# Splitting queries, keys and values into 16-bit halves where they leave PSUM, and turning the keys by DMA when they are loaded

## The chip, the cores and the metric

The kernel runs on one core of one Trainium2 chip. The time is the device time of one execution in microseconds; the kernel before has a median of 2367.46 us over three runs (2366.59 to 2371.02).

## What is computed

One inference step of a decoder with two layers. Layer 0 (the "even" layer) projects the normalised input with one matrix and feeds two mixers with four heads each: a gated linear recurrence (HGRN2, "A") and forgetting attention ("B"). Layer 1 (the "odd" layer) is another gated recurrence (GLA, "C"). There is a prompt of 2048 tokens and a sample of 8 x 4 tokens with a paged cache. The change is in B, for the prompt:

```python
def fox_prompt(q, k, v, log_f):          # (1, 2048, 4 heads, 128)
    c = jnp.cumsum(log_f, axis=1).swapaxes(1, 2)
    def block(args):                     # 128 queries at a time
        qi, ci, s0 = args
        logits = jnp.einsum('bthd,bshd->bhts', qi, k) * scale + ci[..., None] - c[:, :, None, :]
        logits = jnp.where(t[:, None] >= key_pos[None, :], logits, -jnp.inf)
        p = jax.nn.softmax(logits, axis=-1)
        return jnp.einsum('bhts,bshd->bthd', p, v)

def even_mixer(h, w_in, ...):
    qa, fa, ia, ga, qb, kb, vb, gb, fb = _split(h @ w_in, ...)
    o_a, s_a = gated_linear_chunked(...)            # A
    o_b = fox_attend(hb(qb), kb_h, vb_h, log_fb) * jax.nn.silu(gb)   # B
    return jnp.concatenate([o_a, o_b], axis=-1) @ w_out, ...
```

The keys and values kb and vb are outputs too, in float32.

## The kernel before

**Products of two halves.** Float32 data goes through TensorE as two float16 halves: hi = f16(x) and lo = f16(x - hi), scaled by powers of two. A product is three matmuls, hi·hi, hi·lo and lo·hi (`mm3`, lines 595 to 597). Whoever makes an operand must write both halves; `split_evac`, for example, writes hi on ScalarE (ACT) and lo on VectorE (DVE).

**The even layer.** It runs in two halves of 1024 tokens (`hf`; the first takes the 32 sample tokens along). A half is a list of 16 units of the input projection in the order v0, g0, qf0, qf1, Bq0, Bg0, v1, g1, qf2, qf3, Bq1, Bg1, Bk0, Bv0, Bk1, Bv1. A unit holds 256 columns of weights (two heads; Bv0 has four more columns and so a PSUM tile for each 128 tokens instead of one for two). The recurrence of one head (`lin`) is woven between units by `mux`: head 0 beside units 3 and 4, head 1 beside 5 to 7, head 2 beside 9 and 10, head 3 beside 11 to 13, that is Bg1, Bk0 and Bv0. While units 14 and 15 of the first half run, the next half's input is normalised and turned by DMA transposes (L511).

- `mk_bq` (Bq): the projection gives q transposed, head dimension on the partitions, in segments of 352 tokens (first half) or 512 (second). ScalarE copies a segment with the scale `fsc` from PSUM (L990), and SP stores it as float32 to `qTd` in DRAM.
- `mk_bkv` (Bk, Bv): tokens on the partitions. VectorE scales two tiles of 128 tokens into a float32 tile `t` (L1019), which SP stores as the output (L1033). Values are stored a second time to `vd` (L1036). For keys TensorE turns `t` with four transposes (L1044), ScalarE copies them with a scale (L1048, tile `BkS`), and SP stores them to `kTd` (L1050).

PSUM tiles of the projections rotate through three buffers (tag "pj"); `t`, `BkS` and other evacuation tiles share four buffers of 2 KB a partition (tag "c2") with the recurrence's `on`.

**Attention.** `fox_prompt` goes over 16 groups (head h, 512 queries G). For a group `loads` fetches q, k, v (tag "raw", six buffers), the bias row and the gate; `split` makes the halves: ScalarE copies hi (L1330; for v it first scales, L1329), GpSimd (POOL) subtracts to get lo (L1331). In program order the loads of the next group stand after the first block of the present one, the splits of q and k after the third, that of v after the fourth. Then come `scores` (three matmuls a tile, bias and running maximum on VectorE L1384, exponential on ScalarE L1392, normalising on GpSimd L1400) and, one group later, `values`: TensorE transposes of the probabilities (L1420), their halves on ScalarE (`th`, L1427) and VectorE (`tl`, L1428), and three matmuls. `until` weaves this with `fox_sample`, whose pages are loaded by SP (L1514), turned on TensorE (L1544) and copied by VectorE and ScalarE (`kts`).

**Order.** Instructions are traced in program order; a scheduler at compile time then sets the order on each engine by priority, readiness and free buffers. On the chip each engine, and each DMA-issuing queue, takes its instructions strictly in that order. `issue_after` pins an instruction behind another on its engine. The loads of attention are issued by SP, like the pages and nearly all stores.

## Time and profile before

| what | us |
| --- | --- |
| median of three runs | 2367.46 |
| the profiled execution, its own time | 2365.9 |
| its span, first to last instruction | 2364.2 |
| input projection and recurrence of the even layer | 0 to 877 |
| attention, until the prompt's last group | 877 to 1330 |
| output projection of the even layer and the odd layer | 1330 to 2364 |

PE is TensorE's matmul queue and PEld its weight loads, which overlap matmuls; the moving ends of matmuls are modelled, so distances between starts say more than durations. A wait names the instruction that waited and the one that released it, with the total, the number of times and the longest. The granted TensorE clock of the execution is 0.989. A view by windows gives for each stretch its length and then the busy time of each engine with the number of instructions; restricted to one line, it gives that line's busy time alone.

### The profile page before, as it was taken

The page shows a single profiled execution, that of the slowest core. Times are in us where ns is not written, and L with a number is a line of the kernel's source. Part 1 is how long each engine was busy: PE and PEld are TensorE (multiplying, and loading weights), DVE is VectorE, ACT ScalarE, POOL GpSimd, SP SyncE. Part 2 cuts the span into 40 slices and gives each one's busy share as a digit, 9 for nine tenths or more (in the row PEclk, how much of TensorE's full clock was granted, in tenths as well). Part 3 has the DMA queues.
Part 4 walks back from the last instruction along what each step waited for, and adds up shares of the span by engine and source line. Part 5 has one row for each costly group of instructions (what it writes and reads, how often), then busy time and mean ns, then how long its engine had stood idle before and what let it go on. Part 6 is the DMA issues. An engine that isn't in the chain of part 4 may idle for free. (4 is left out here: it accounts for less than half of the span.)

```text
span 2364.2 us, 58202 instructions
## 1 busy us (share of the span) xinstructions
PE 2265.2 (96%) x23124; PEld 1613.1 (68%) x23124; DVE 1404.4 (59%) x3225; ACT 1090.3 (46%) x2372; POOL 818.6 (35%) x858
## 2 busy tenths in 40 slices
PE   6999999999999999999999999999899999999998
PEld 5667667864655875655445888777677666666887
DVE  6656557536664538666767444366675655557554
ACT  5434343333333226556667543436545545545333
POOL 3133324112212226234557345144452422222223
PEclk9999999999999999999999999999999999999999
DMA  6231334755441267776873867633234431115453
GB/s 191 73 89 59 100 109 146 196 157 148 145 123 56 75 196 239 239 256 198 280 239 117 278 197 249 148 96 108 79 117 101 107 103 57 48 55 166 152 194 149
DMA packets 358004, 344.89 MB, mean 146 GB/s; under 512 B 90994, under 2 KB 300723, under 8 KB 357731
## 3 DMA queue, kind: packets, MB, share of 16 engines
q1 hardware_dynamic: 356226, 336.64, 46.8%
q8 instruction: 182, 2.98, 0.5%
q0 software_dynamic: 1504, 4.52, 0.5%
q14 instruction: 92, 0.75, 0.1%
HBM read 248.73 MB, written 79.63 MB: 139 GB/s over the span
## 5 line engine op out<-in xcount | busy, mean ns | idle before, releaser
L595 PE MATMUL pt_o<-w_o,act 128*128 128x256 f16 x1024 | 281.1, 274 | 8.2 <-DVE xo L1825 6.6
L597 PE MATMUL pt_o<-w_o,act 128*128 128x256 f16 x1024 | 281.0, 274 | 3.8 <-DVE act L1784 3.7
L596 PE MATMUL pt_o<-w_o,act 128*128 128x256 f16 x1024 | 281.1, 275 | 1.5 <-POOL w_o L356 1.5
L597 PEld LDWEIGHTS <-act 128*128 128x128 f16 x2304 | 227.3, 99 | 39.4 <-DVE act L1784 5.1
L596 PEld LDWEIGHTS <-act 128*128 128x128 f16 x2304 | 227.3, 99 | 38.5 <-issue 8.4
L595 PEld LDWEIGHTS <-act 128*128 128x128 f16 x2304 | 227.4, 99 | 35.9 <-issue 3.4
L761 POOL TENSOR_TENSOR kA<-kA,fA 128x512 f32<-128x512 f32 (+1 forms) x56 | 79.5, 1419 | 190.1 <-PE gl_A L727 141.9
L595 PE MATMUL pt_Cv<-w_Cv,act 128*128 128x256 f16 (+1 forms) x512 | 141.4, 276 | 0.0
L597 PE MATMUL pt_Cv<-w_Cv,act 128*128 128x256 f16 (+1 forms) x512 | 141.3, 276 | 0.0
L596 PE MATMUL pt_Cv<-w_Cv,act 128*128 128x256 f16 (+1 forms) x512 | 141.3, 276 | 0.0
L761 POOL TENSOR_TENSOR kC<-kC,fC 128x512 f32<-128x512 f32 (+1 forms) x56 | 83.6, 1493 | 153.8 <-PE gl_C L727 102.5
L1392 ACT ACTIVATE L<-L,nm,kc 128x512 f32<-128x512 f32 (+3 forms) x160 | 118.2, 741 | 33.5 <-DVE nm L1390 27.8
L1400 POOL TENSOR_SCALAR L<-L,nm 128x512 f32<-128x512 f32 (+3 forms) x160 | 99.0, 632 | 64.5 <-DVE nm L1396 23.9
L1427 ACT ACTIVATE th<-pt 128x512 f16<-128x512 f32 (+3 forms) x159 | 80.5, 528 | 64.5 <-PE pt L1420 63.6
L1428 DVE TENSOR_TENSOR tl<-pt,th 128x512 f16<-128x512 f32 (+3 forms) x159 | 94.6, 609 | 21.4 <-ACT th L1427 20.5
L1420 PE MATMUL pt<-ident,L 128*128 128x128 f32 x544 | 91.2, 279 | 7.1 <-POOL L L1400 4.2
L1420 PEld LDWEIGHTS pt<-ident,L 128*128 128x128 f32 x544 | 66.6, 143 | 33.3 <-DVE tl L1428 8.3
L1544 PEld LDWEIGHTS pkt<-ident,pgcache_fox_k 128*128 128x128 f32 x512 | 57.4, 141 | 42.7 <-issue 25.1
L1877 ACT ACTIVATE vC<-pt_Cv,kc 128x512 f32<-128x512 f32 (+1 forms) x40 | 23.9, 598 | 129.9 <-PE pt_Cv L597 129.9
L1544 PE MATMUL pkt<-ident,pgcache_fox_k 128*128 128x128 f32 x512 | 75.1, 278 | 7.3 <-DVE kts L1548 5.1
L1825 DVE SCALAR_TENSOR_TENSOR xo<-pt_o,kc,xo 128x512 f32<-128x512 f32 x48 | 35.8, 748 | 62.0 <-PE pt_o L597 57.2
L597 PE MATMUL pt_Av<-w_Ai,act 128*128 128x256 f16 x256 | 70.9, 277 | 1.5 <-DVE act L591 1.5
(957 smaller groups left out, 6788.5 us busy)
## 6 DMA issues: line engine op xcount, KB each, us to landing
pgcache_fox_k<-in_cache_fox_k SPq DMA_DIRECT2D x128, 256.0 KB, 4.4
pgcache_fox_v<-in_cache_fox_v SPq DMA_DIRECT2D x128, 256.0 KB, 4.3
yr<-yT SPq DMA_DIRECT2D x16, 1024.0 KB, 7.2
x1d<-xo SPq DMA_DIRECT2D x48, 256.0 KB, 4.1
wr_Aqf<-in_w_in_even SPq DMA_DIRECT2D x64, 128.0 KB, 3.2
wr_o<-in_w_out_even SPq DMA_DIRECT2D x32, 256.0 KB, 6.0
xo<-in_x_prompt SPq DMA_DIRECT2D x32, 256.0 KB, 4.2
wr_Cv<-in_w_in_odd SPq DMA_DIRECT2D x32, 256.0 KB, 3.8
```

The source lines that it names most:

```text
L595: nc.tensor.matmul(ps, lh[0], rh[0], start=first, stop=False)
L596: nc.tensor.matmul(ps, lh[0], rh[1], start=False, stop=False)
L597: return nc.tensor.matmul(ps, lh[1], rh[0], start=False, stop=last)
L761: nc.gpsimd.tensor_tensor(kv[:, :, 0], kv[:, :, 0], t1.to_broadcast([P, nb, w]), ALU.mult)
L1392: self.last_exp = nc.scalar.activation(lt[:, :w], lt[:, :w], AF.Exp, bias=nm[:, 0:1], scale=ib, accum_out=nm[:, 2 + j : 3 + j])
L1400: nc.gpsimd.tensor_scalar(lt[:, :w], lt[:, :w], nm[:, 1:2], 2.0**14, ALU.mult, ALU.mult)
L1420: nc.tensor.transpose(pt[:, w : w + P], rows[b][s // 4][0][:, (s % 4) * P : (s % 4 + 1) * P], self.ident)
L1427: nc.scalar.activation(th[:, a:w], pt[:, a:w], AF.Copy),
L1428: nc.vector.tensor_tensor(tl[:, a:w], pt[:, a:w], th[:, a:w], ALU.subtract)))
L1544: nc.tensor.transpose(pk[:, j * P : (j + 1) * P], pgs[j][:, h * P : (h + 1) * P], self.ident)
L1825: nc.vector.scalar_tensor_tensor(t[:m, :cnt], ps, c, t[:m, :cnt], ALU.mult, ALU.add)
L1877: r = nc.scalar.activation(v[h][:, g : g + cnt], ps[:, :, :256], AF.Copy, scale=c)
```

## The change

- **Queries** (`mk_bq`): a segment is written to an f16 tile with hi and lo side by side, hi by ScalarE, lo by VectorE from PSUM, and stored to `qd`. The sample's 32 queries, in the last segment of the first half, get a float32 tile and store of their own.
- **Keys and values** (`mk_bkv`): beside the float32 tile, which stays for the outputs, a second tile `u` takes hi (ScalarE) and lo (VectorE) of each 128-token tile with the scale `cu`, and is stored to `kd` or `vd`, tokens as rows. The transposes of prompt keys and their copy go; those of the 32 sample keys stay.
- **Loading** (`loads`): q and v are loaded as halves, k by a DMA transpose of 512 rows of 256 f16 values (hi and lo of one head). `load` and `split` go. Three buffers for q, six each for k and v.
- **Scales** (`fox_scale`): one more small product `cu` for keys and values.

```diff
-        self.qTd = dp.tile([NH, P, NTOK], F32, name="qTd")
-        self.kTd = dp.tile([NH, P, NTOK], F32, name="kTd")
+        self.qd = dp.tile([NH, P, 2, T], F16, name="qd")
+        self.kd = dp.tile([T, NH, 2, P], F16, name="kd")
+        self.vd = dp.tile([T, NH, 2, P], F16, name="vd")
...
                         if which == "q":
-                            nc.scalar.activation(t[:, :m], ps, AF.Copy, scale=self.fsc["q", hp][0])
-                            store_cols(self.qTd[h], t, c0, m)
+                            up, few = self.fsc["q", hp][0], max(0, c0 + m - HALF)
+                            u = t.bitcast(F16).rearrange("p (x t) -> p x t", x=2)[:, :, : m - few]
+                            nc.scalar.activation(u[:, 0], ps[:, : m - few], AF.Copy, scale=up)
+                            nc.vector.scalar_tensor_tensor(u[:, 1], ps[:, : m - few], up, u[:, 0], ALU.mult,
+                                                           ALU.subtract)
+                            dc = hf * HALF + c0
+                            nc.sync.dma_start(self.qd[h][:, :, dc : dc + m - few], u)
+                            if few:
+                                t = wp.tile([P, 512], F32, tag="c2", name=f"BqS{h}")[:, :few]
+                                nc.scalar.activation(t, ps[:, m - few :], AF.Copy, scale=up)
+                                nc.sync.dma_start(self.qs[h], t)
...
                         held[:] = [wp.tile([P, 2, 256], F32, tag="c2", name=f"B{which}{hf}{hp}{g}")]
+                        if m == P:
+                            held.append(wp.tile([P, 512], F32, tag="c2", name=f"B{which}s{hf}{hp}{g}").bitcast(
+                                F16).rearrange("p (g h x d) -> p g h x d", g=2, h=2, x=2))
                     t = held[0]
                     nc.vector.tensor_scalar(t[:m, g % 2 : g % 2 + cnt], ps[:, :, :256], c, None, ALU.mult)
+                    if m == P:
+                        u = held[1]
+                        for j in range(cnt):
+                            src = ps[:, j, :256].rearrange("p (h d) -> p h d", h=2)
+                            hi, lo = (u[:, g % 2 + j, :, x] for x in range(2))
+                            nc.scalar.activation(hi, src, AF.Copy, scale=self.cu[which, hp])
+                            nc.vector.scalar_tensor_tensor(lo, src, self.cu[which, hp], hi, ALU.mult, ALU.subtract)
...
-                        if which == "v":
-                            dst = self.vd[pg * P : (pg + 2) * P, cs].rearrange("(g s) d -> s g d", s=P)
-                            nc.sync.dma_start(dst, t)
-                    else:
-                        return
-                    if which == "k":
+                        dst = {"k": self.kd, "v": self.vd}[which][pg * P : (pg + 2) * P, 2 * hp : 2 * hp + 2]
+                        nc.sync.dma_start(dst.rearrange("(g s) h x d -> s g (h x d)", s=P),
+                                          u.rearrange("p g h x d -> p g (h x d)"))
+                    if which == "k" and m < P:
...
-            fx = Pool(f0, {"vh": 5, "vl": 5, "P": 17, "th": 4, "tl": 4, "sg": 3, "y": 1},
-                      Pool(f1, {"raw": 6, "caus": 1, "qh": 2, "ql": 2, "kh": 5, "kl": 5, "cb": 2, "st1": 12, "cm": 2}))
+            fx = Pool(f0, {"v2": 6, "P": 17, "th": 4, "tl": 4, "sg": 3, "y": 1},
+                      Pool(f1, {"caus": 1, "q2": 3, "k2": 6, "cb": 2, "st1": 12, "cm": 2}))
...
         def loads(h, G):
             gs = slice(G * 512, (G + 1) * 512)
-            raw["q"] = self.load(fx, self.qTd[h][:, gs], f"q{h}{G}")
-            raw["k"] = self.load(fx, self.kTd[h][:, gs], f"k{h}{G}")
+            q, k, v = (fx.tile([P, 1024], F16, tag=x + "2", name=f"{x}2_{h}{G}") for x in "qkv")
+            q, k = (x.rearrange("p (x t) -> p x t", x=2) for x in (q, k))
+            v = v.rearrange("p (c x d) -> p c x d", c=4, x=2)
+            nc.sync.dma_start(q, self.qd[h][:, :, gs])
+            nc.sync.dma_start_transpose(k, self.kd[gs, h].rearrange("t x d -> t (x d)"))
             bias(h, G)
-            raw["v"] = self.load(fx, self.vd[gs, h * P : (h + 1) * P].rearrange("(c s) d -> s c d", s=P), f"v{h}{G}")
+            nc.sync.dma_start(v.rearrange("p c x d -> p c (x d)"),
+                              self.vd[gs, h].rearrange("(c s) x d -> s c (x d)", s=P))
...
-        for x in "qkv":
-            split(x, 0, 0)
...
-                if j + 1 < len(groups):
-                    if b == 0:
-                        loads(*groups[j + 1])
-                    elif b == 2:
-                        split("q", *groups[j + 1])
-                        split("k", *groups[j + 1])
-                    elif b == 3:
-                        split("v", *groups[j + 1])
+                if j + 1 < len(groups) and b == 0:
+                    loads(*groups[j + 1])
...
         nc.vector.reciprocal(up, down)
+        self.cu[which, hp] = self.kcol()
+        nc.vector.tensor_scalar(self.cu[which, hp], c, up, None, ALU.mult)
```

More of the change, by code (lines that the diff above doesn't have):

```diff
@@ L152, in consts @@
         dp = self.ctx.enter_context(self.tc.tile_pool(name="scr", bufs=1, space=DRAM))
-        self.qTd = dp.tile([NH, P, NTOK], F32, name="qTd")
-        self.kTd = dp.tile([NH, P, NTOK], F32, name="kTd")
+        self.qd = dp.tile([NH, P, 2, T], F16, name="qd")
+        self.kd = dp.tile([T, NH, 2, P], F16, name="kd")
+        self.vd = dp.tile([T, NH, 2, P], F16, name="vd")
+        self.qs = dp.tile([NH, P, TS], F32, name="qs")
+        self.ks = dp.tile([NH, P, TS], F32, name="ks")
+        self.vs = dp.tile([TS, 512], F32, name="vs")
         self.sgd = dp.tile([NH, P, NTOK], F32, name="sgd")
-        self.vd = dp.tile([NTOK, 512], F32, name="vd")
         self.cbd = dp.tile([NH, T], F32, name="cbd")
@@ L1023, in ev @@
                         if which == "v":
-                            nc.sync.dma_start(self.vd[T : T + TS, cs], t[:m, 0])
+                            nc.sync.dma_start(self.vs[:, cs], t[:m, 0])
                     elif (g + cnt) % 2 == 0:
@@ L1033, in ev @@
                         nc.sync.dma_start(dst, t)
-                        if which == "v":
-                            dst = self.vd[pg * P : (pg + 2) * P, cs].rearrange("(g s) d -> s g d", s=P)
-                            nc.sync.dma_start(dst, t)
-                    else:
-                        return
-                    if which == "k":
+                        dst = {"k": self.kd, "v": self.vd}[which][pg * P : (pg + 2) * P, 2 * hp : 2 * hp + 2]
+                        nc.sync.dma_start(dst.rearrange("(g s) h x d -> s g (h x d)", s=P),
+                                          u.rearrange("p g h x d -> p g (h x d)"))
+                    if which == "k" and m < P:
                         pk = pps.tile([P, 2, 256], F32, tag="gr", name=f"BkT{hf}{hp}{g}")
-                        nt = 1 if m < P else 2
                         for j in range(2):
-                            for c in range(nt):
-                                nc.tensor.transpose(pk[:, j, c * P : c * P + m], t[:m, c, j * P : (j + 1) * P],
-                                                    self.ident[:m, :m])
+                            nc.tensor.transpose(pk[:, j, :m], t[:m, 0, j * P : (j + 1) * P], self.ident[:m, :m])
                         ks = wp.tile([P, 2, 256], F32, tag="c2", name=f"BkS{hf}{hp}{g}")
-                        wd = nt * m
-                        nc.scalar.activation(ks[:, :, :wd], pk[:, :, :wd], AF.Copy, scale=self.fsc["k", hp][0])
-                        dc = T if m < P else hf * HALF + g * P
-                        nc.sync.dma_start(
-                            self.kTd[2 * hp : 2 * hp + 2, :, dc : dc + wd].rearrange("h p t -> p h t"), ks[:, :, :wd])
+                        nc.scalar.activation(ks[:, :, :m], pk[:, :, :m], AF.Copy, scale=self.fsc["k", hp][0])
+                        nc.sync.dma_start(self.ks[2 * hp : 2 * hp + 2].rearrange("h p t -> p h t"), ks[:, :, :m])
                 yield from self.proj_tm(pps, act, W, hf, ev, f"B{which}{hf}{hp}", width)
@@ L1087, in phase_even @@
             self.early, self.last_ev = set(), None
-            self.scales2, self.ready, self.fsc, self.logit, self.v_undo = {}, {}, {}, {}, {}
+            self.scales2, self.ready, self.fsc, self.logit, self.v_undo, self.cu = {}, {}, {}, {}, {}, {}
             self.sx_even = self.gain_scale(self.g_even, pps, "pj", "e")
@@ L1315, in phase_fox @@
                 drain(until(self.prompt, FOX_P, self.fox_sample(fs, pps), FOX_S))
-    def load(self, fx, src, nm):
-        r = fx.tile([P, 512], F32, tag="raw", name=f"raw_{nm}")
-        self.nc.sync.dma_start(r.rearrange("p (c d) -> p c d", d=src.shape[2]) if len(src.shape) == 3 else r, src)
-        return r
-    def split(self, fx, r, nm, scale=None):
-        nc = self.nc
-        hi = fx.tile([P, 512], F16, tag=nm[0] + "h", name=f"h_{nm}")
-        lo = fx.tile([P, 512], F16, tag=nm[0] + "l", name=f"l_{nm}")
-        if scale is not None:
-            nc.scalar.activation(r, r, AF.Copy, scale=scale)
-        nc.scalar.activation(hi, r, AF.Copy)
-        nc.gpsimd.tensor_tensor(lo, r, hi, ALU.subtract)
-        return hi, lo
     def fox_prompt(self, fx, pps, caus):
         nc = self.nc
-        cbs, K, V, Q, SG, raw = {}, {}, {}, {}, {}, {}
+        cbs, K, V, Q, SG = {}, {}, {}, {}, {}
         self.turns = []
@@ L1349, in loads @@
             gs = slice(G * 512, (G + 1) * 512)
-            raw["q"] = self.load(fx, self.qTd[h][:, gs], f"q{h}{G}")
-            raw["k"] = self.load(fx, self.kTd[h][:, gs], f"k{h}{G}")
+            q, k, v = (fx.tile([P, 1024], F16, tag=x + "2", name=f"{x}2_{h}{G}") for x in "qkv")
[3 more added lines that the diff above has]
+            nc.sync.dma_start_transpose(k, self.kd[gs, h].rearrange("t x d -> t (x d)"))
             bias(h, G)
-            raw["v"] = self.load(fx, self.vd[gs, h * P : (h + 1) * P].rearrange("(c s) d -> s c d", s=P), f"v{h}{G}")
+            nc.sync.dma_start(v.rearrange("p c x d -> p c (x d)"),
+                              self.vd[gs, h].rearrange("(c s) x d -> s c (x d)", s=P))
+            Q[h, G], K[h, G], V[h, G] = ([x[:, 0], x[:, 1]] for x in (q, k, v.rearrange("p c x d -> p x c d")))
             SG[h, G] = fx.tile([P, 512], F32, tag="sg", name=f"fsg{h}{G}")
             nc.sync.dma_start(SG[h, G], self.sgd[h][:, gs])
-        def split(which, h, G):
-            with ExitStack() as st:
-                for x in (self.last_exp, self.last_kt):
-                    if x is not None:
-                        st.enter_context(self.tc.issue_after(x.ins))
-                r = self.split(fx, raw[which], f"{which}{h}{G}", self.fsc["v", h // 2][0] if which == "v" else None)
-                {"q": Q, "k": K, "v": V}[which][h, G] = r
         def scores(h, G, b):
@@ L1437, in values @@
                 for s, a, c0 in parts:
-                    vv = [x[:, (s % 4) * P : (s % 4 + 1) * P] for x in V[h, s // 4]]
+                    vv = [x[:, s % 4] for x in V[h, s // 4]]
                     self.last_pe = self.mm3(po[:, c0:c2], vv, [x[:, a : a + c2 - c0] for x in (th, tl)], s == 0,
@@ L1524, in fox_sample @@
         vn = one([TS, 512], "vn")
-        for t, d in ((qs, self.qTd), (kn, self.kTd), (sgs, self.sgd)):
-            nc.sync.dma_start(t, d[:, :, T : T + TS].rearrange("h p t -> p h t"))
-        nc.sync.dma_start(vn, self.vd[T : T + TS])
+        for t, d in ((qs, self.qs), (kn, self.ks), (sgs, self.sgd[:, :, T : T + TS])):
+            nc.sync.dma_start(t, d.rearrange("h p t -> p h t"))
+        nc.sync.dma_start(vn, self.vs)
         with self.tc.issue_after(self.last_l.ins):
```

## The prediction

> **What bounds the kernel now.** I read the page of the profile first, then the busy time of each engine by stage, then the waits of TensorE, and last the instructions of the lines that the change touches.

> ```profile
> span 2364.2 us, 58202 instructions
> ...
> PE 2265.2 (96%) x23124; PEld 1613.1 (68%) x23124; DVE 1404.4 (59%) x3225; ACT 1090.3 (46%) x2372; POOL 818.6 (35%) x858
> ```

> TensorE is idle for 99 us of the span in all, so time can come only from TensorE work that is left out, from those 99 us, or from new stalls. The stages that the change touches, each row giving its start and end, its length, and then the busy time of PE, PEld, DVE, ACT and POOL:

> ```profile
> 358.00:485.00 127.00, 124.32 (x1439) 107.94 (x1438) 74.95 (x155) 41.76 (x89) 34.77 (x28) 0.99 0.67 180
> ...
> 760.00:877.00 117.00, 113.12 (x1354) 95.90 (x1352) 56.44 (x130) 26.00 (x68) 24.29 (x28) 0.99 0.40 121
> 877.00:1330.00 453.00, 423.51 (x3052) 256.01 (x3052) 312.95 (x944) 296.23 (x660) 228.77 (x334) 0.98 0.72 232
> ```

> The first two are the key and value projections (units Bk and Bv) of the two halves, the third is attention. The projections leave TensorE idle for 2.7 and 3.9 us: there, removed TensorE work is worth its full length, and relief for any other engine is worth nothing. Attention leaves it idle for 29.5 us. What ended the longer of these idle times (total, times, longest):

> ```profile
> PE pkt L1544 <- DVE kts L1548: 5.1, 6, 1.7
> PE pt L1420 <- POOL L L1400: 4.2, 4, 2.3
> PE fo L595 <- ACT th L1427: 3.3, 4, 1.8
> PE fo L596 <- DVE tl L1428: 2.8, 4, 1.3
> PE pt L1420 <- DVE tl L1428: 2.7, 9, 0.5
> ...
> PE s L596 <- POOL l_k L1331: 1.2, 2, 0.7
> ...
> PE s L597 <- POOL l_q L1331: 0.4, 1, 0.4
> ```

> No row names a DMA. Attention is therefore held by many short waits on three engines, VectorE first.

> **The change, part by part.**

> *The key transposes leave TensorE.* L1044 turns each pair of 128-token key tiles with four f32 transposes, 16 pairs in all. One pair in its surroundings, then all of L1044 up to 877 us (PE, then PEld):

> ```profile
> 842.37 0.27 PE L597 MATMUL pt_Bk<-w_Bk,act 128*128 128x256 f16 x1
> 842.48 0.60 PE L1044 MATMUL BkT<-ident,Bk 128*128 128x128 f32 x4
> 842.91 0.27 PE L595 MATMUL pt_Bk<-w_Bk,act 128*128 128x256 f16 x1
> ...
> 0.00:877.00 877.00, 10.75 (x68) 7.87 (x68) 0.99 0.42 122
> ```

> The next matmul starts 0.43 us after the first transpose started, so a pair holds the queue for 0.43 us, and 16 pairs for 6.9 us. The upper bound is the busy sum of 10.75 us, which counts overlapping ends and the four small sample transposes that stay. I take 7.0, because the gap between starts is what the following work sees.

> *New evacuation in the projections.* The pair's ScalarE copy (L1048, 16 of 512 columns) goes. For k and v alike, each 128-token tile gets a ScalarE copy to f16 from PSUM (256 columns) and a VectorE scalar_tensor_tensor for the rest: 64 of each. Queries keep their ScalarE copy (L990) and gain 20 VectorE operations, 12 of at most 352 columns and 8 of 512. The nearest rows, the first four with count, busy time and mean ns (the Bk row with min/median/max):

> ```profile
> L1048 ACT ACTIVATE BkS<-BkT,kc 128x512 f32<-128x512 f32 x3 | 2.1, 687 | 15.0 <-PE BkT L1044 15.0
> ...
> L1427 ACT ACTIVATE th<-pt 128x256 f16<-128x256 f32 x15 | 5.6, 376 | 9.5 <-PE pt L1420 9.5
> ...
> L1019 DVE TENSOR_SCALAR Bv<-pt_Bv,kc 128x256 f32<-128x256 f32 x8 | 3.7, 475 | 0.0
> ...
> L1019 DVE TENSOR_SCALAR Bk<-pt_Bk,kc x16: 731/750/751, 369.2 to 851.1; 128x512 f32<-128x512 f32 x16
> ```

> ScalarE: 64 x 0.376 - 16 x 0.687 = +13 us. VectorE: 64 x 0.475 = 30 us, and for the queries 8 x 0.75 + 12 x 0.58 (between the two rows by width) = 13 us: +43 us. It lies beside matmuls: a pair of tiles takes about 48 x 0.11 = 5.3 us of TensorE, and its VectorE work grows from 0.75 to 1.70 us, with three buffers ("pj") to cover it. The cover has one thin place, the wide value unit Bv0 of the first half:

> ```profile
> 400.00:410.00 10.00, 9.65 (x82) 8.58 (x81) 9.77 (x26) 3.32 (x13) 3.31 (x3) 1.00 0.56 172
> 410.00:420.00 10.00, 10.00 (x93) 8.98 (x92) 9.42 (x24) 6.60 (x16) 3.09 (x4) 1.00 0.57 174
> 420.00:430.00 10.00, 10.00 (x110) 8.64 (x108) 8.85 (x19) 5.13 (x9) 3.85 (x4) 1.00 0.84 269
> ...
> PE o_A L881 <- DVE Sx L887: 1.7, 4, 0.6
> ```

> VectorE is busy for 28.0 of these 30 us. Each new `lo` also waits for ScalarE's `hi` at the head of VectorE's queue; behind it stand the state updates of the recurrence (L887), for which TensorE already waits (last row, of the whole even layer). Cost in TensorE time: 0 if the buffers cover all of it. The other end is the 24 `lo` of the units that run beside the fourth head's recurrence (Bk0 twice, Bv0 of the first half) with VectorE more than three quarters busy: 24 x (0.475 + 0.376) = 20 us if all is passed on. I take 2.0, near the lower end, because TensorE lost only 1.7 us on that very wait and 0.35 us in the densest 30 us. The straddling query segments add four small ScalarE copies and four stores, under the same cover.

> *Splits leave attention.* Sixteen groups lose L1329 (scaling v), three L1330 (hi) and three L1331 (lo). Busy time over 840 to 1330 us, in that order:

> ```profile
> 840.00:1330.00 490.00, 11.37 (x16) 0.98 0.71 229
> ...
> 840.00:1330.00 490.00, 28.25 (x48) 0.98 0.71 229
> ...
> 840.00:1330.00 490.00, 55.09 (x48) 0.98 0.71 229
> ```

> ScalarE loses 39.6 us, GpSimd 55.1 us. Neither is the bound, so only the waits count. The waits on `l_k` and `l_q` vanish: 1.6 us. Of those on GpSimd's L1400 and ScalarE's `th` (4.2 + 3.3 = 7.5) some come from a split standing in front in the queue. Bounds: 0 and 7.5, and with what VectorE inherits from ScalarE (`tl` follows `th`, 5.5) 13.0; a loss is excluded, since nothing is added to these two engines. I take 4.0, about half of the direct waits. What is late next is VectorE, which loses no work.

> *The entry into attention.*

> ```profile
> 874.22 0.22 PE L595 MATMUL s<-h_k,h_q 128*128 128x128 f16 x1 [0.99 <-DVE Bv L1019]
> ```

> The first score matmul waits for the last value tile's evacuation. Two `lo` operations now follow that evacuation before the buffer is free: 2 x 0.475 = 0.95. I add 1.0; the lower bound is 0, if the first score takes another buffer.

> *Loads.* Bytes are the same. The 16 key loads become DMA transposes of 256 KB on SP's queue; the page loads of the sample stand behind them. The kernel's present transposes have 512 KB each. First their issue on SP (ns), then the issue of the present key load, then the DMA share and GB/s (last two columns) with and without transposes:

> ```profile
> L511 SPq DMA_TRANSPOSE act<-xhl x8: 1662/2472/3547, 451.6 to 476.5; - x8
> ...
> DMA to landing us min/median/max: 3.8/5.2/7.1
> ...
> L1320 SPq DMA_DIRECT2D raw_k<-kTd x16: 332/372/428, 860.2 to 1217.3; - x16
> ...
> 460.00:470.00 10.00, 10.00 (x94) 8.90 (x92) 2.65 (x4) 0.00 (x0) 0.00 (x0) 1.00 1.19 253
> ...
> 890.00:900.00 10.00, 6.58 (x46) 3.96 (x47) 9.63 (x28) 6.79 (x15) 7.34 (x10) 1.00 0.97 335
> ```

> At most 16 x (3.5 - 0.4) = 50 us more of SP, by the median 34, by half the bytes 14. The DMA engines need 4.2 MB / 253 GB/s = 16.6 us instead of 4.2 / 335 = 12.5. I cost both at nothing. A key tile is loaded one group ahead, TensorE waits for no DMA in attention, and the first one, issued near 860 us, is there by 860 + 3.5 + 7.1 = 871, before 874.22. If that cover went, every one of 16 groups could wait up to the extra issue time: 50 us at worst.

> [...]

> **The sum.** 2365.9 (the profiled execution's own time, span 2364.2 plus 1.7) - 7.0 - 1.6 - 4.0 + 2.0 + 1.0 = 2356.3. The profiled execution lies 1.6 us under the median of the runs, 2367.46, so I predict a median of 2357.5, 0.4% less. With the bounds of the terms around it the forecast's own range is 2349 to 2362.

> **The rivals.**

> *More comes out of attention.* GpSimd's splits may slow VectorE itself. In one stretch VectorE's two `kn` operations took 2.31 us, the two equal `qs` before them 0.61, and the former ended with the GpSimd splits:

> ```profile
> 892.29 0.61 DVE L1532 TENSOR_SCALAR qs<-qs,kc 128x64 f32<-128x64 f32 x2
> 892.83 2.31 DVE L1532 TENSOR_SCALAR kn<-kn,kc 128x64 f32<-128x64 f32 x2
> ...
> 892.82 1.16 POOL L1331 TENSOR_TENSOR l_q<-raw_q,h_q 128x512 f16<-128x512 f32 x1
> 893.92 1.16 POOL L1331 TENSOR_TENSOR l_k<-raw_k,h_k 128x512 f16<-128x512 f32 x1
> ```

> With the splits gone the waits on VectorE (5.1 + 2.8 + 2.7 = 10.6) could largely go too, and the waits on `th` and L1400 in full (3.5 beyond my 4.0): 2357.5 - 10.6 x 0.7 - 3.5 = 2347. Against it: most of the VectorE work on which TensorE waits reads PSUM, unlike `kn`. [...]

> *The gain is eaten.* VectorE's backlog in the even layer costs 6 us instead of 2 and attention's order of work, made anew around the missing splits, gives nothing but the 1.6: 2357.5 + 4 + 4 = 2365.5, no change that can be told. For it: 28.0 of 30 us. Against it: after 430 us VectorE has slack to catch up (75 of 127 us in that stage).

> *Slower: the `lo` operations hold VectorE's queue.* The place is the fourth head's recurrence beside Bk0 and Bv0. If each of the 24 `lo` passes its time and its wait for `hi` on to TensorE, that is the 20 us of above instead of 2, and with attention's 4.0 not realised: 2357.5 + 18 + 4 = 2379.5. It decides from about 15 us passed on. For it: GpSimd's and VectorE's part of that recurrence is a chain. Against it: 0.35 us lost by TensorE where VectorE was 93% busy.

> *The key tiles come late*, so that the change trades TensorE transposes for waits on DMA. A median issue of 2.5 us, 16 times, of which half is seen: 2357.5 + 20 = 2377.5. Against it: the loads lead by a group.

> **How the numbers follow.** Forecast 0.52; more out of attention 0.11; gain eaten 0.16; VectorE's queue 0.14; late keys 0.07. What a measurement can tell from no change is about 0.2%, 4.7 us, so faster means below 2362.7 and slower above 2372.2. Nearly all of the first two is faster: 0.62. Within: 0.17. Slower: 0.21. The range for 8 in 10 leaves out the lower half of the second case and most of the slower ones: 2345 to 2374.

> **What would show it.** No L1044 of 128 rows and TensorE busy some 7 us less before 877 us; VectorE about 43 us busier there, with the waits of `o_A` on `Sx` as the measure of the 2 us. In attention no L1329 to L1331 work, ScalarE 40 and GpSimd 55 us less busy, and TensorE idle for 24 instead of 29.5 us. The forecast is wrong if TensorE waits for a DMA of `k2`, if the stages to 877 us end less than 3 us earlier, or if attention takes longer than before.

## The result and the profile after

The changed kernel takes 2388.72 us, median of four runs (2386.38 to 2392.97), beside 2369.24 for the kernel before on the same chip: a ratio of 1.0087, 95% interval 1.0071 to 1.0103, some 20 us slower. The forecast was 2357.5, its range ended at 2374. The profiled execution took 2386.38 us. First the page's head, span and busy time by engine:

```profile
span 2384.7 us, 58132 instructions
...
PE 2254.9 (95%) x23060; PEld 1606.7 (67%) x23060; DVE 1444.0 (61%) x3313; ACT 1074.2 (45%) x2360; POOL 762.4 (32%) x810
```

TensorE is busy 10 us less and the span is 20 us longer: idle time went from 99 to 130 us. The other engines' sums moved in the forecast's direction: VectorE +40 us, ScalarE -16, GpSimd -56. None of that is where the time went. The stages of the prediction, in the same columns, and one stretch late in attention:

```profile
358.00:485.00 127.00, 121.05 (x1402) 103.15 (x1401) 87.37 (x193) 50.70 (x115) 37.20 (x31) 0.99 0.65 173
760.00:877.00 117.00, 109.42 (x1331) 92.44 (x1328) 69.03 (x153) 32.31 (x87) 20.39 (x24) 0.99 0.44 125
877.00:1330.00 453.00, 407.14 (x2907) 246.73 (x2908) 306.14 (x934) 246.90 (x565) 167.47 (x279) 0.97 0.72 223
...
1200.00:1320.00 120.00, 93.68 (x632) 49.88 (x633) 69.63 (x185) 53.28 (x120) 43.11 (x60) 0.96 0.79 251
```

Attention leaves TensorE idle for 453.0 - 407.1 = 45.9 us where it was 29.5, and 26 of these lie in the 120 us of the last row, with the DMA engines four fifths busy. What ended the waits in attention (total, times, longest):

```profile
PE pv L1668 <- DMA pgcache_fox_v<-in_cache_fox_v: 20.0, 14, 2.9
PE s L598 <- DVE mx L1377: 14.5, 5, 8.7
PE fo L599 <- DVE tl L1421: 6.2, 5, 3.5
PE pt L1413 <- DVE tl L1421: 3.8, 1, 3.8
...
PE pkt L1529 <- DVE kts L1533: 1.6, 2, 0.8
PE fo L598 <- ACT th L1420: 1.5, 2, 0.8
```

Of the waits that the forecast counted, most have shrunk (`kts` 5.1 to 1.6, `th` 3.3 to 1.5, those on GpSimd's L1400, on `l_k` and on `l_q` no longer show), but those on `tl` have grown, from 2.8 + 2.7 to 6.2 + 3.8. Above them stand two rows that no part of the sum foresaw: TensorE waits 20.0 us for the sample's value pages, and 14.5 us for the row maxima of the first scores, 8.7 of it in one piece.

By the first and last instructions of each kind, the first score starts at 869.8 instead of 874.2, the last `fo` starts at 1314.9 instead of 1299.2, and the rest from there lasts 1069.8 instead of 1065.0: -4.4 in the even layer, +20.1 in attention, +4.8 behind it.

**The pages.** The sample's work on TensorE by stretch, `pkt` (turns of key pages) of before, then of after; the count stands behind the first busy time:

```profile
890.00:1100.00 210.00, 75.12 (x512) 57.43 (x512) 44.03 (x64) 37.88 (x64) 1.00 0.70 231
1100.00:1200.00 100.00, 0.00 (x0) 0.00 (x0) 0.00 (x0) 0.00 (x0) 1.00 0.81 263
```

```profile
890.00:1100.00 210.00, 60.61 (x404) 47.53 (x404) 34.35 (x50) 29.91 (x51) 0.99 0.68 207
1100.00:1200.00 100.00, 15.95 (x108) 12.45 (x108) 9.60 (x14) 7.83 (x14) 1.00 0.64 201
```

Before, all 512 turns were done by 1100 us. After, 108 are left, so the value pages, which come behind the key pages, are asked for some 50 us later (SP issues them from 1107 to 1278 us instead of 1054 to 1231). The prompt has run ahead meanwhile; its score matmuls `s` up to 1100 us, of 480 in all, before and then after:

```profile
860.00:1100.00 240.00, 55.03 (x228) 52.56 (x97) 0.99 0.73 240
```

```profile
860.00:1100.00 240.00, 66.14 (x275) 63.69 (x120) 0.96 0.73 219
```

Later there is less prompt work to do while a page is on its way, and TensorE waits. The two streams of attention, prompt and sample, have lost their pace.

**The entry.** TensorE, VectorE and SP where attention begins:

```profile
874.19 0.32 PE L598 MATMUL s<-k,q 128*128 128x384 f16 x1 [3.75 <-DVE mx L1377]
...
883.56 0.61 PE L598 MATMUL s<-k,q 128*128 128x512 f16 x1 [8.72 <-DVE mx L1377]
```

```profile
882.70 0.29 DVE L1377 CUSTOM_DVE_ANT_0 L<-s,cb 128x128 f32<-128x128 f32 x1 [8.31 <-DMA vd<-Bvs]
```

```profile
870.11 1.93 SPq L1351 DMA_TRANSPOSE k<-kd  x1
...
875.28 0.58 SPq L1055 DMA_DIRECT2D out_fox_v_p<-Bv  x1
...
878.11 0.96 SPq L1499 DMA_DIRECT2D pgcache_fox_k<-in_cache_fox_k  x2
879.17 0.38 SPq L1057 DMA_DIRECT2D vd<-Bvs  x1
```

VectorE wants to write the second logits tile and waits 8.3 us for a store of `Bvs`, the f16 parts of the last two value tiles, which have been ready since 873.9 but whose store SP issues at 879.17, behind the sample's loads and two pages. Why should logits wait for that store? In the compiled kernel's memory map the second logits tile lies at bytes 119296 to 121344 of each partition, and the last `Bvs` at 119648. Before, it lay at 125440, clear of all projection tiles: the buffers ahead of it in attention's pool are 6 KB smaller after the change.

### The profile page after: what moved, and what is told of

Its sections match the earlier page's. It is cut to its first block, busy times and chain, and to the rows that moved or that the text cites. A ratio compares the mean times of both kernels' runs of the same rounds, so it can differ in the third digit from the quotient of the medians.

```text
span 2384.7 us, 58132 instructions
## 1 busy us (share of the span) xinstructions
PE 2254.9 (95%) x23060; PEld 1606.7 (67%) x23060; DVE 1444.0 (61%) x3313; ACT 1074.2 (45%) x2360; POOL 762.4 (32%) x810
## 4 chain that ended last, share of the span: by engine, by line
PE 46%; DVE 5%; DMA 5%; issue 2%; ACT 2%; POOL 1%; SPq 1%; DVEq 0%; POOLq 0%; ACTq 0%
PE pt_o L598 3%; PE pt_o L599 3%; PE pt_o L600 3%; PE pkt L1529 2%; PE pt L1413 2%; PE pt_Cv L598 2%; PE pt_Cv L599 2%; PE pt_Cv L600 2%; DMA pgcache_fox_v<-in_cache_fox_v 2%; PE sc L1587 1%; DMA yr<-yT 1%; PE pv L1668 1%; PE gl_C L730 1%; PE o_C L884 1%; PE fo L599 1%
## 5 line engine op out<-in xcount | busy, mean ns | idle before, releaser
L1420 ACT ACTIVATE th<-pt 128x512 f16<-128x512 f32 (+3 forms) x159 | 82.2, 530 | 114.6 <-PE pt L1413 113.8
L1421 DVE TENSOR_TENSOR tl<-pt,th 128x512 f16<-128x512 f32 (+3 forms) x159 | 95.0, 609 | 28.7 <-ACT th L1420 27.3
L1413 PEld LDWEIGHTS pt<-ident,L 128*128 128x128 f32 x544 | 64.9, 141 | 27.3 <-DVE tl L1421 6.7
L1363 POOL TENSOR_TENSOR cm<-cb,caus 128x128 f32<-128x128 f32 x64 | 29.1, 456 | 155.1 <-DVE mx L1377 94.5
```

The costliest lines, as they stand in the source:

```text
L1363: self.last_cm = nc.gpsimd.tensor_tensor(cm, cb[:, tb * P : (tb + 1) * P], caus, ALU.add)
L1413: nc.tensor.transpose(pt[:, w : w + P], rows[b][s // 4][0][:, (s % 4) * P : (s % 4 + 1) * P], self.ident)
L1420: nc.scalar.activation(th[:, a:w], pt[:, a:w], AF.Copy),
L1421: nc.vector.tensor_tensor(tl[:, a:w], pt[:, a:w], th[:, a:w], ALU.subtract)))
```

## The experiments

Each run is given by its ratio to the kernel before on the same chip, with the 95% interval; 0.1% is 2.4 us. Three suspects: the lost pace (A), the entry (C to G), the transposing loads (B, H, I, J). The letters are those of the expectations. A fourth question is what the removed splits were worth.

### Pace

p1 is the kernel *before* with one pin less. The removed inner function `split` put its instructions behind two others on ScalarE, the last exponential and the sample's latest copy of turned key pages:

```
-                for x in (self.last_exp, self.last_kt):
+                for x in (self.last_exp,):
```

> The kernel before, in which a group's splits are pinned behind the last exponential only and no longer behind the sample's latest copy of turned key pages. Theory A (that pin paced the prompt against the sample; without it the prompt runs ahead, and the sample's value pages are all asked for at the end): TensorE waits 10 to 25 us for value pages in attention, where it waited for no page before, and the time is 2379 to 2394 us. Theory B (the new work of the change makes it slower: transposing key loads, the VectorE operations, the entry): no wait on pages, 2369 us within 5.

Ratio 1.0067 (1.0051 to 1.0084), median 2381.07. The waits on TensorE in attention, first row:

```profile
PE pv L1683 <- DMA pgcache_fox_v<-in_cache_fox_v: 20.5, 15, 2.8
```

The same wait at the same size, with none of the change's new work, and the prompt is as far ahead (282 score matmuls by 1100 us). p2 puts a pin back into the kernel *after*, on TensorE, since ScalarE has no splits there to pin:

```
+                with ExitStack() as st:
+                    if b == 0 and j == 0 and self.gate is not None:
+                        st.enter_context(self.tc.issue_after(self.gate.ins))
                     self.last_pe = self.mm3(...)
...
+                if b == 2:
+                    self.gate = self.last_pkt
```

> The kernel after, with the pacing put back by other means: the first scores of each group are pinned on TensorE behind the turn of the sample's key pages that was the latest at block 2 of the group before. Theory A: the wait of pv on value pages falls from 20.0 us to under 3, and the time from 2388.7 to between 2368 and 2375 us; the entry into attention (waits of 8.7 and 3.8 us) stays as it is. Theory B: nothing changes, 2389 us within 5.

Ratio 1.0059 (1.0038 to 1.0081): 2378.13, less regained than expected. All 512 key turns are done by 1100 us again, with 225 score matmuls beside them; the wait on pages is gone as it should be, and the entry stands:

```profile
PE s L598 <- DVE mx L1381: 16.5, 9, 9.0
...
PE pv L1676 <- DMA pgcache_fox_v<-in_cache_fox_v: 2.9, 1, 2.9
```

A wait that ends is not all time won: 17 us of page waits went, and attention in p2's profile is 441.2 us where it was 445.1.

s4 is the cleanest test of pace: the later kernel s1 (below), with the entry cured, without the gate.

> s1 without the gate: the loss of pace alone. Theory A: waits of about 20 us for value pages come back, and the time is 8 to 16 us over s1. Rival: with the entry cleared, the sample keeps up by itself, and the time is that of s1 within 3.

1.0072 (1.0044 to 1.0099) against s1's 1.0018 (1.0004 to 1.0033): 0.54% or 13 us for the gate alone, and the page waits are back at 17.5 us. Between q1 and q2 (below) the gate is worth 0.41%. The lost pace is shown as a cause, from both sides: p1 makes the loss, the gate takes it back.

### The entry

p4 is p2 with the last value unit's stores on ScalarE's queue:

```
+                        eng = nc.scalar if (which, hp, hf) == ("v", 1, 1) else nc.sync
+                        eng.dma_start(dst.rearrange(...), u.rearrange(...))
```

> The kernel of p2, in which the last value unit's stores of the f16 parts go out on ScalarE's DMA queue instead of SP's. Theory C (the wait of 8.7 us at the entry into attention is for the last of these stores, which stands on SP's queue behind the sample's loads, two pages and a transposing load, while the first logits want the memory of its tile): the waits of 8.7 and 3.8 us fall to about 2 in all, and the time is 8 to 10 us under that of p2. Rival D (another wait, for the store of the f32 page or for the key load, ends at nearly the same time): the time is that of p2 within 3 us.

A miss: 1.0085 (1.0067 to 1.0102), and the wait was 10.0 us. ScalarE's queue brought the last store out only at 877.67, though its tile had been full since 871.4. The trace shows what held it:

```profile
877.67 0.37 ACTq L1058 DMA_DIRECT2D vd<-Bvs  x1
878.09 0.49 ACT L1390 ACTIVATE L<-L,nm,kc 128x128 f32<-128x128 f32 x1 [7.25 <-DMA cb<-cbd]
```

ScalarE stood idle until one of SP's loads of a bias row had landed; in the compiled program the store waits for that load, which counts on the same semaphore. So the store came out no earlier than in p2 (877.6), and what the other queue is worth stays untested. VectorE waited for this same store again, 9.6 us, which speaks for C.

q1 leaves the stores alone and moves the logits, by giving them a pool of their own behind the others:

```
-            fx = Pool(f0, {"v2": 6, "P": 17, "th": 4, "tl": 4, "sg": 3, "y": 1},
+            fx = Pool(f0, {"P": 17}, Pool(f2, {"v2": 6, "th": 4, "tl": 4, "sg": 3, "y": 1}),
```

> The kernel after, without the gate of p2, in which the logits' tiles (P) come last in attention's memory, 10 KB higher, so that the logits of the first four 128-row blocks no longer lie where the last value tiles and their f16 parts lay. Theory C2 (the second logits wait for the store of the last f16 parts only because the change made the buffers ahead of them 6 KB smaller and so moved them onto that tile): the wait of 8.7 us at the entry falls under 2, the waits for value pages stay at about 20, and the time is 8 to 12 us under after's: 2375 to 2381 us beside a before of 2367. Rival E (the entry waits for the DMA engines, which are busy with six transposing loads there): the wait stays above 5 us, the time within 4 us of after's.

1.0074 (1.0050 to 1.0097), only 0.13% under after's ratio, though the wait of 8.7 us at the entry is gone; the longest there is now 5.9 us, of the kind shown at q2 below, and the waits on value pages stayed at 20.1. A likely reading is that a sample that is late anyway takes back what the entry gives. q2 has both:

> p2 (the gate) and q1 (the logits high) together. Theories A and C2 add up: no wait on value pages above 3 us in all, none above 2 at the entry, and 8 to 12 us less than p2, 2362 to 2368 us, level with before or up to 4 us under it. Rival E: as p2, 2374 to 2380 us.

1.0033 (1.0021 to 1.0046): 0.26% or 6 us under p2, less than the 8 to 12 expected. The entry's 9.0 are gone; 5.2 remain, of another kind:

```profile
870.57 0.47 ACT L1040 ACTIVATE Bvs<-pt_Bv,kc 128x256 f16<-128x256 f32 x1 [6.25 <-DMA vd<-Bvs]
```

ScalarE cannot begin the last pair's f16 parts, because all four buffers of the projections' output tiles, of which a pair now takes two, wait for their stores. q3 has six:

```
-EC2 = 4
+EC2 = 6
```

> q2 with six instead of four buffers for the projections' output tiles, of which the change takes two instead of one per pair of value tiles. If their number holds back ScalarE and VectorE at the end of the value projection (waits up to 4.8 us on the store of an f16 tile), the first scores' blocks begin 1 to 4 us earlier and the time falls by as much; if not, it is that of q2 within 2 us.

1.0035 (1.0019 to 1.0052), no gain in the time. In its trace that wait is gone and the entry's is 2.7 us, but one of 5.6 us stands at 886 us, where the eighth logits tile (s1's expectation miscounts it as the twelfth) still overlaps the last f16 tile by 352 bytes and the compiled program waits for its store (the trace names a page that SP issued half a microsecond ahead of that store). r3 is q2 with SP's later loads and pages held behind the last store of value parts (`issue_after` on that store):

> q2, in which SP issues the loads of the second group on, the sample's loads and the pages behind the last store of value parts. In q2 the last value pair's f16 parts began 6.2 us late, because ScalarE waited for the store of two pairs earlier to free its tile, which stood on SP among transposing loads. Theory F (order on SP and the engines' load at the entry): the wait of 5.2 us at the entry falls to 2.7 or less, and the time by 2 to 4 us under q2's, 2369 to 2371. Rival: what is held comes late in its turn, a wait of as much or more appears on the loads of the second group or on the pages, and the time is that of q2 or up to 6 us over it.

1.0027 (1.0012 to 1.0043): the entry's longest wait is 2.7 us as expected, the time is q2's within the intervals. The reverse test is r1, the kernel *before* with its `l_v` tiles moved behind the logits, which brings the logits down by 5 KB:

```
-            fx = Pool(f0, {"vh": 5, "vl": 5, "P": 17, "th": 4, "tl": 4, "sg": 3, "y": 1},
+            fx = Pool(f0, {"vh": 5, "P": 17, "th": 4, "tl": 4, "sg": 3, "y": 1}, Pool(f2, {"vl": 5}),
```

> The kernel before, with the 5 KB of value parts l_v moved behind the logits in attention's memory, so that the second and third logits lie on the last value tiles, as they do after the change, and nothing else changed. Theory C2 (place in memory): a wait of 4 to 10 us appears on the entry's scores, and the time is 4 to 10 us over before's. Rival E (the DMA engines, busy with transposing loads, which are not here): no wait above 1.5 us, the time as before within 3 us.

1.0021 (1.0004 to 1.0039), about 5 us, and the wait appears in a kernel with no transposing key load, though shorter than expected (2.9 us on VectorE, 3.3 on TensorE):

```profile
877.85 0.29 DVE L1385 CUSTOM_DVE_ANT_0 L<-s,cb 128x128 f32<-128x128 f32 x1 [2.92 <-DMA vd<-Bv]
```

So the place in memory makes the wait by itself. It is shorter than after's because the tile beneath is that of the last pair but one, whose store SP had issued at 872.51. s1 takes q3 and moves the logits up by 4.5 KB more, so that the first ten tiles lie clear of the last value tiles (the expectation's fifteen is too many: the eleventh lies on the last f16 tile, and no wait shows there):

```
+            nc.gpsimd.memset(f2.tile([P, 1152], F32, tag="gap", name="gap", bufs=1)[:, :1], 0.0)
```

> q3 with the logits' tiles another 4.5 KB higher, so that none of the first fifteen lies on the projections' last tiles. In q3 the twelfth logits tile still did, and TensorE waited 5.6 us at 886 us. Theory G (with pace and place put right, the change brings what the prediction summed, except what the transposing loads cost beside them): no wait over 3 us in the first 30 us of attention; 2366 to 2370 us beside a before of 2365. Rival H (the transposing loads slow attention throughout): the time stays at q3's 2373 to 2376, with the waits spread over attention.

1.0018 (1.0004 to 1.0033). The waits in its attention:

```profile
PE s L598 <- DVE mx L1383: 6.1, 9, 2.7
PE pt L1419 <- POOL L L1399: 4.1, 2, 3.8
PE fo L598 <- ACT th L1426: 3.7, 7, 1.6
PE pv L1678 <- DMA pgcache_fox_v<-in_cache_fox_v: 3.3, 1, 3.3
```

With pace, place and buffers put right, about 16 of the 20 us are explained. The two causes hide behind each other: alone, the entry's cure is worth 0.15% (after against s4, inside the intervals) and the gate 0.28% (after against p2); as the second of the two, the entry's cure is worth 0.41% (p2 against s1) and the gate 0.54%. Run once more beside t1, it came out lower still:

> s1 once more, beside t1 on the same chip. Its first profile had a rest after attention of 1072.1 us against 1065.0 of before with the same number of matmuls, and more stretches of a lowered clock. If that belongs to the kernel, it comes again, and the ratio is 1.0018 again; if it was chance, the rest is 1065 within 3 and the ratio nearer 1.000.

1.0008 (0.9994 to 1.0021), while the rest after attention in its profile was 1078.6 us: longer, not shorter, than in s1's first. That profile is of the slowest of its twelve executions, 2379.02 us. Both expectations were half right; more on the rest stands below.

### The transposing loads

p3 is *after* with the keys turned by TensorE again, split from PSUM, stored turned and loaded plainly:

```
+                        for j in range(2):
+                            for c in range(2):
+                                nc.tensor.transpose(pk[:, j, c * P : c * P + P], t[:, c, j * P : (j + 1) * P], self.ident)
...
-            nc.sync.dma_start_transpose(k, self.kd[gs, h].rearrange("t x d -> t (x d)"))
+            nc.sync.dma_start(k, self.kd[h][:, :, gs])
```

> The kernel after, but the keys are again turned by TensorE in the projections (128-row transposes, one ScalarE and one VectorE operation per pair of tiles make the two f16 parts from PSUM), stored turned, and loaded by plain DMAs; no pin. Theory A: attention stays as long as after (445 us, waits on value pages about 20 us), and the even layer gets the 5 to 7 us back that the transposes cost: 2392 to 2397 us. Theory B, with the transposing loads as what is late: attention falls to about 430 us, and the time to 2375 to 2382 us.

1.0101 (1.0076 to 1.0125). Attention took 438.5 us with 21.3 us of waits on value pages, so theory B fell; but the first score came at 886.3, 16.5 us late, more than the turns' 7 (r4, with six output buffers instead of four, has it at 878.2). r4 and s2 are the same edit on q3 and on s1:

> q3 with the keys turned by TensorE and loaded by plain DMAs, as in p3. If the transposing loads are what is left of the loss (theory B on the rest): attention and what follows get 5 to 10 us shorter and the even layer 7 longer, 2371 to 2376 beside q3's 2374. If they cost nothing, the even layer's 7 us are simply lost: 2380 to 2383, with attention as in q3.

> r4 (keys turned by TensorE, plain loads, gate, six tiles) with the logits 4.5 KB higher as in s1. Theory G: the 8 us of the even layer that s1 has ahead of it stay lost, 2365 to 2368, within 3 us of s1 either way. Rival H: 6 or more us under s1, 2362 to 2366.

r4: 1.0007 (0.9992 to 1.0022); s2: 1.0009 (0.9993 to 1.0026), both level with before. r4 against q3 looked like a price of 6 us on the transposing loads, but q3 had its logits tile on a late store and r4, by its other allocation, had not; s2 against s1, where neither has, leaves 0.09%, well inside the intervals. s2's first score is at 876.5, s1's at 869.4: 7.1 us of lead that s1 does not keep. By the starts of the same score matmuls the lead is 2.9 us at 892 and gone at 936 (s2 has the 101st at 934.2, s1 at 935.6). The first 30 us of attention, s1's row first, then s2's:

```profile
869.40:899.40 30.00, 22.96 (x131) 13.42 (x129) 22.81 (x91) 16.71 (x42) 13.51 (x29) 0.89 1.03 299
```

```profile
876.50:906.50 30.00, 24.66 (x153) 14.30 (x151) 26.09 (x101) 18.44 (x46) 15.56 (x37) 0.94 1.00 324
```

The DMA engines are full in both (shares of 1.03 and 1.00), and in 30 us s1 does 131 matmuls where s2 does 153. A likely reading is that whoever enters earlier finds less of what it needs in memory: up to 936 us s1 waits 2.5 us for key pages, s2 0.6. t1 separates the turning itself: s1's program with plain loads of the same bytes, so that the keys are left unturned.

```
-            nc.sync.dma_start_transpose(k, self.kd[gs, h].rearrange("t x d -> t (x d)"))
+            nc.sync.dma_start(k.rearrange("p x t -> p (x t)").rearrange("p (c y) -> p c y", c=4),
+                              self.kd[gs, h].rearrange("(c s) x d -> s c (x d)", s=P))
```

> s1 with the sixteen transposing key loads replaced by plain loads of the same bytes: the keys are not turned, so the scores are not those of the reference; all else, the order on every engine among it, is s1's. Theory I (the transposing loads cost what the even layer gains: longer on SP, longer on the DMA engines): 5 to 9 us under s1, about 2362 beside a before of 2367, with the sixteen issues on SP at 0.4 instead of 1.3 to 2.6 us. Theory J (they cost nothing once the entry is clear): s1 within 2 us.

1.0005 (0.9992 to 1.0018) against 1.0008 (0.9994 to 1.0021) for s1 on the same chip. The issues on SP, s1 again and then t1 (ns, min/median/max):

```profile
L1354 SPq DMA_TRANSPOSE k<-kd x16: 1223/1281/2967, 853.2 to 1202.1; - x16
```

```profile
L1354 SPq DMA_DIRECT2D k<-kd x16: 359/412/860, 850.9 to 1197.5; - x16
```

0.9 us more per issue, 14 us of SP in all, and no cost that can be told (by the intervals, one of up to some 4 us could hide): theory J. On ScalarE's queue instead (`nc.scalar.dma_start_transpose`) they do cost:

> s1 with the transposing key loads issued from ScalarE's queue instead of SP's. If their price is the issue time on SP (1.3 to 2.6 us each, with all other loads behind them): 3 to 7 us under s1. If it is the DMA engines' time: s1 within 2 us, or up to 5 over it where ScalarE's own work waits behind an issue.

1.0092 (1.0067 to 1.0117). ScalarE's own work stands behind the issues, two of which held it for 6.8 us in the middle of the value projection, and the first score came at 879.1.

### What the splits were worth

r2 puts idle splits into q2: per group four ScalarE copies and three GpSimd subtractions into tiles that nobody reads.

```
+                if j + 1 < len(groups) and b >= 2:
+                    for x in ("qk", "v")[b - 2]:
...
+                            if x == "v":
+                                nc.scalar.activation(hi, r, AF.Copy)
+                            nc.scalar.activation(hi, r, AF.Copy)
+                            nc.gpsimd.tensor_tensor(lo, r, hi, ALU.subtract)
```

> q2 with the removed load on ScalarE and GpSimd put back as idle work: for each group four ScalarE copies of a 128x512 tile (three to f16, one more for v) and three GpSimd subtractions, into tiles that nobody reads, at the places and behind the exponential where the splits stood. Step of the prediction (the splits' departure saves 4.0 us of waits in attention): 3 to 6 us over q2's 2373. Rival (TensorE's waits in attention do not come from these two engines): q2 within 2 us.

1.0075 (1.0047 to 1.0102), 10 us over q2, but spoilt: the tile they read came late and ScalarE waited 11.2 us for it once. s3 reads another, on s1:

> s1 with the idle ScalarE and GpSimd work of r2 (four copies and three subtractions per group). In r2 they read a tile that was loaded late, and ScalarE waited 11.2 us for it; here they read one of the group at hand, long in memory. Step of the prediction (the splits' departure saves 4.0 us): 3 to 6 us over s1. If the 12 us of r2 were the splits' own price: 9 to 14 over s1. If these engines do not matter: within 2.

1.0054 (1.0032 to 1.0075), 0.36% or 8.5 us over s1, the two intervals just touching; one such wait of 4.6 us is still in it. If that wait counts in full, 4 us are the splits' own.

## Why the prediction was wrong, step by step

**The step that failed is the one on the splits**: "only the waits count", with the bounds 0 and 13.0 and "a loss is excluded, since nothing is added to these two engines". It took the splits as load on two engines. They were also the carrier of an order: `split` was where the prompt's next group was held behind the sample's key pages. With the instructions went the pin, and TensorE, which had waited for no page, waited 20.0 us for them. The waits on `tl`, which stood in the upper bound as something to gain, grew by 4.5 us. The gate gives 0.28% to 0.54% back, and taking the pin alone from the kernel before costs 0.67%. The kernel's text had it in plain sight; the prediction read the lines as work only.

**The size of the gain in that step was fair.** s3 puts it at 4 to 8.5 us, and attention of s2, with plain loads and the gate, is 4.6 us shorter than before (420.4 against 425.0, one profile each). The sum had 4.0 + 1.6.

**The entry was mis-sized.** The sum had +1.0 for two `lo` operations. Before, the first scores' waits were 0.99 and 0.47 + 0.32; after, 3.75 and 8.72: +10.7 us. In s1, with memory and buffers in order, they are 2.69 + 0.32, +1.2, so the `lo` were priced rightly. What was missing: which tiles the logits inherit memory from (r1), and that a pair of value tiles now fills two of four buffers (q2 against q3's trace).

**The transposes off TensorE were right.** -7.0 was forecast; TensorE's busy time in the two projection stages fell by 3.3 + 3.7 us, and s1 and s2, which differ in who turns the keys, are 7.1 us apart at the first score. Of the sum's -5.0 up to there, -7.0 + 2.0, the measured -4.4 came, 1.0 of it by a wait of the first score that moved to a later one. But the lead was not kept where attention begins with full DMA engines. That it does so stood in the rows of before (share 0.97, 335 GB/s), where they were read as a rate only.

**VectorE's `lo` in the even layer** was right: the waits of `o_A` on the recurrence's state (L887 before, L890 after) went from 1.7 to 3.4 us, within a start that came 4.4 earlier.

**The loads at nothing** was right, though for s1 only once the rest was cured: t1 differs by 0.03%. No TensorE wait in after names a key tile. The issue on SP took 1.28 us where the plain load's took 0.41.

**The rivals.** The late keys did not come. The `lo` at the recurrence did not hold VectorE. More out of attention by way of GpSimd: the row on which it rested did change, twice 1.19 us before, 0.24 now, and with s3's idle splits one of the two is at 1.19 again (after, then s3):

```profile
L1517 DVE TENSOR_SCALAR kn<-kn,kc x2: 243/243/243, 897.3 to 897.5; 128x64 f32<-128x64 f32 x2
```

```profile
L1535 DVE TENSOR_SCALAR kn<-kn,kc x2: 241/716/1192, 891.0 to 892.1; 128x64 f32<-128x64 f32 x2
```

So that operation, 0.24 us long without GpSimd's splits, took 0.95 us more with them in the kernel, twice before and once in s3. But the VectorE work on which TensorE waits reads PSUM, and it did not get faster; `tl`, busy time and mean ns, before and then after:

```profile
L1428 DVE TENSOR_TENSOR tl<-pt,th 128x512 f16<-128x512 f32 x112 | 75.6, 686 | 20.3 <-ACT th L1427 19.6
```

```profile
L1421 DVE TENSOR_TENSOR tl<-pt,th 128x512 f16<-128x512 f32 x112 | 75.3, 686 | 21.0 <-ACT th L1420 20.0
```

The rivals that ended slower were given 0.21 in all, and neither's mechanism was the one that came. The list of what would show the forecast wrong did catch it: "if attention takes longer than before".

**The range.** The terms' bounds, added up as they stand, give 2342 to 2380 (the loads at nothing), not the 2349 to 2362 that is called the forecast's own range, and the sum with the 1.6 gives 2357.9, not 2357.5. The wider range does not reach the result either, since the lost pace is no term of it.

**What stays open.** By the sum, s1 should lie 10 us under before; it lies 2 to 4 over. Part is the lead lost at the entry. The rest after attention, with 11149 matmuls in each of these profiles, lasts 1072.1 and 1078.6 us in s1's two, 1065.9 in s2's, 1065.0 before, and 1055.4 in p1's. Of the 7.1 and 13.6 us that s1's lie over before, TensorE's stretches at half clock account for about 5.1 and 6.8 by an estimate that counts half their length (23.9 and 27.3 us of them in the rest, against 13.7) and the waits on `xo` for 3.2 and 7.0 (9.8 and 13.6, against 6.6). Why the waits on `xo` grow no run here says. No version was faster than the kernel before; r4, s2, t1 and s1's second run are level with it.

## What to carry to other kernels

An instruction that is removed may be the peg on which an order hangs: ask of each removed line not only what it cost but what was issued behind it, and which stream it held back. When buffers change size, look at which old tiles the first tiles of the next stage come to lie on, since here a logits tile waited for the last store from its place, 8.3 us after and 2.9 us in r1. And time saved just ahead of a stage that begins with its loads outstanding may be lost again there, as s1's lead of 7.1 us was by 936 us.

## What the hardware showed beside that

```profile
2176.38 0.72 PE L727 MATMUL gl_C<-qC,kC 128*30 128x16 f32 x64 [1.95 <-DVE sam_o L634]
```

```profile
2172.62:2176.04 3.42, 1.81 (x17) 1.38 (x15) 3.26 (x10) 0.00 (x0) 0.00 (x0) 1.00 0.68 228
2176.04:2179.45 3.41, 3.07 (x87) 2.82 (x88) 3.29 (x9) 0.00 (x0) 1.49 (x1) 1.00 0.25 78
```

```profile
2185.51 0.72 PE L730 MATMUL gl_C<-qC,kC 128*30 128x16 f32 x64 [1.95 <-DVE sam_o L637]
```

```profile
2182.93:2186.35 3.42, 1.47 (x72) 1.15 (x71) 3.24 (x8) 0.00 (x0) 0.00 (x0) 1.00 0.54 162
2186.35:2189.76 3.41, 3.41 (x18) 2.45 (x17) 3.25 (x8) 0.00 (x0) 1.51 (x1) 0.50 0.23 77
```

Before, the wait ran over the window's end, TensorE was idle for 47% of the first window, and the clock stayed at 1.00; in s1 the whole wait fell into one window, 57% idle, and the next ran at 0.50. A wait of 2.69 us that ended at 1429.58 in the same run lay across two windows (idle for 50% and 29%), and no drop followed. By the modelled ends, 18 of the 22 drops behind the first 50 us of these two profiles follow a window idle for 57% or more, and from there on no window at full clock was idle for as much without a drop behind it; four drops, after windows idle for 39% to 53%, do not fit. Executions of one kernel spread over 10 us and more (t1: 2360.59 to 2373.44), and waits that fall into one window in one execution and across two in another are one likely reason, which no run tests.
